# A two-layer hybrid backbone on one core: merged triangular inverses, attention in units of two heads, and separate buffers for the first weights of layer 1

## The chip, the core and the metric

The kernel runs on one core of one Trainium2 chip. The metric is the device time of one execution, in microseconds (us). The engines are TensorE (PE in the profile; its weight loads are PEld), VectorE (DVE), ScalarE (ACT), GpSimd (POOL) and SyncE (SP). Each works through its own queue in order.

## The reference

Two layers act on 512 latent tokens and 256 context tokens of width 1024, in float32. Each layer normalises and modulates the tokens, projects them once, and gives the columns to three mixers whose outputs are concatenated and projected out; then a feed-forward network (layer 0) or a top-2-of-8 mixture of experts (layer 1) follows. In layer 1 only the latents are carried on. The two mixers that the change touches:

```python
# attention: 8 query heads, 2 key/value heads of width 64
s = jnp.einsum('bqkgd,bskd->bkgqs', qi, k).astype(F32) * scale
p = jax.nn.softmax(s, axis=-1).astype(v.dtype)
return jnp.einsum('bkgqs,bskd->bqkgd', p, v)
...
# gated delta rule, 4 heads, chunks of 64, forward and backward
lower = jnp.where(strict, beta[..., :, None] * kk * decay, 0.0)
sol = lax.linalg.triangular_solve(jnp.eye(cs, dtype=F32) + lower, rhs,
                                  left_side=True, lower=True, unit_diagonal=True)
```

Latents attend to all 768 tokens, context tokens (layer 0 only) to the 256 of the context.

## The kernel before, in words

Full-precision products are made of three matmuls of operands that were split into a high and a low part (`parts`, L205: ScalarE writes the high part, VectorE subtracts for the low one). `weights` (L166) opens the buffers for raw and split weights, `load` (L193) has SyncE fetch one, `split` (L199) splits it. Per layer the program runs as follows.

1. `project` (L575) makes the projections: the head columns of three groups (`heads`, `group`; matmuls L220 to L222), channel columns (`feat`; L214 to L216), the gates and the gram matrices of the delta rule. In layer 0 the first group's weights are loaded in advance; in layer 1 they are loaded in `heads(1, w0)`, with `w0` empty, into the buffers that `k.weights(es, 5, pa, 2)` opens. These lie where the residual stream x of the feed-forward part was.
2. `solve` (L1521) inverts the unit triangular 32x32 blocks of all chunks and heads. `solve1` (L1661) does one direction: four 32x1024 transposes (L1672) bring the blocks into one lane each (`tt`), then for each of 30 pivots a multiply (L1681) and an add (L1682) follow, then a 128x1024 transpose back (L1685). The two directions are run in step (`zip`), so their instructions alternate. They all have a high priority in the scheduler.
3. Attention is a generator (L1432) of which one step is run after every second (layer 0) or third (layer 1) pivot, and the rest during the delta-rule steps. One step takes one head and one pair of query tiles of 128: `scores` (L1473) makes S on TensorE (L1483, L1484), VectorE takes the row maximum (L1485) and negates it (L1486), ScalarE takes the exponential with the row sums (L1487), VectorE the reciprocal (L1488), and P is multiplied by it, on VectorE (L1490) or ScalarE (L1492) as `DVE_SCALE` says. `values` (L1451) works one step later: transposes of P (L230), copies of them (L1457), products with V in two column halves of the array (L1461), the sum of the two halves (L1464 on ScalarE, L1466 on VectorE). Query tiles: 48 in layer 0 (8 heads x 6), 32 in layer 1 (8 x 4).
4. `merge` (L1703) builds 64x64 inverses, and `stage2` (L1739) runs the 12 steps of the delta rule in both directions: r (L1777, or for a chunk by a GpSimd-issued transfer L1778), products with the inverse (L1784), the decay matrices (L1800, on GpSimd in layer 0) and so on. Steps of attention stand between them.
5. `tail` projects out and runs the feed-forward part.

A tile scheduler fixes the order of instructions on each engine when the program is built, from priorities; buffers come from pools, and an instruction waits until its buffer's last reader is done.

## Time and profile before

| | |
|---|---|
| median of 3 runs | 2194.21 us (2187.08 to 2195.78) |
| the profiled execution | 2191.7 us |
| span of its trace | 2190.1 us |
| TensorE busy | 2033.4 us (93%) |
| VectorE busy | 1473.6 us (67%) |
| ScalarE busy | 1010.3 us (46%) |
| GpSimd busy | 157.5 us (7%) |
| mean granted TensorE clock | 0.970 |

Busy times are averages over stages with different limits, so the change is to be read in its own stages: projections and inverses of layer 0 to about 275 us, its merge and delta-rule steps to 446, the start of layer 1 at 1126 to 1157, its inverses to 1390 and its steps to 1497. A TensorE record can contain waiting, since matmuls are pipelined and their ends are modelled.

### The profile page before, as it was taken

The page shows a single profiled execution, that of the slowest core. Times are in us where ns is not written, and L with a number is a line of the kernel's source. Part 1 is how long each engine was busy: PE and PEld are TensorE (multiplying, and loading weights), DVE is VectorE, ACT ScalarE, POOL GpSimd, SP SyncE. Part 2 cuts the span into 40 slices and gives each one's busy share as a digit, 9 for nine tenths or more (in the row PEclk, how much of TensorE's full clock was granted, in tenths as well). Part 3 has the DMA queues.
Part 4 walks back from the last instruction along what each step waited for, and adds up shares of the span by engine and source line. Part 5 has one row for each costly group of instructions (what it writes and reads, how often), then busy time and mean ns, then how long its engine had stood idle before and what let it go on. Part 6 is the DMA issues. An engine that isn't in the chain of part 4 may idle for free. (4 is left out here: it accounts for less than half of the span.)

```text
span 2190.1 us, 33735 instructions
## 1 busy us (share of the span) xinstructions
PE 2033.4 (93%) x12390; PEld 1647.6 (75%) x12390; DVE 1473.6 (67%) x2857; ACT 1010.3 (46%) x1764; POOL 157.5 (7%) x226
## 2 busy tenths in 40 slices
PE   6999999988999999999969997899889999999995
PEld 2988766776888888888849875677667777777774
DVE  4859967766885624242366599787667788766776
ACT  3664386633322222222235544753455576655554
POOL 0000201100000000000000003110020000000011
PEclk9999999999999999999979999998999999999998
DMA  6332544152554515131313223106597799667783
GB/s 259 98 120 64 170 159 159 36 190 80 185 193 153 179 29 198 48 97 44 107 33 103 97 89 94 40 30 210 178 267 274 238 353 347 208 234 231 245 289 127
DMA packets 120755, 342.47 MB, mean 156 GB/s; under 512 B 13104, under 2 KB 34592, under 8 KB 120576
## 3 DMA queue, kind: packets, MB, share of 16 engines
q1 hardware_dynamic: 80064, 271.75, 36.9%
q0 software_dynamic: 15248, 49.97, 6.8%
q10 hardware_dynamic: 25264, 18.42, 2.7%
q8 instruction: 106, 1.74, 0.3%
q14 instruction: 73, 0.60, 0.1%
HBM read 304.95 MB, written 35.14 MB: 155 GB/s over the span
## 5 line engine op out<-in xcount | busy, mean ns | idle before, releaser
L206 ACT ACTIVATE hi<-raw 128x1024 fp32r<-128x1024 f32 (+3 forms) x444 | 426.5, 986 | 333.9 <-PE ps L215 255.2
L207 DVE TENSOR_TENSOR lo<-raw,hi 128x1024 fp32r<-128x1024 f32 (+3 forms) x444 | 494.9, 1134 | 90.7 <-ACT hi L206 76.8
L214 PE MATMUL ps<-hh,hi 128*128 128x512 f32 (+1 forms) x1040 | 356.3, 343 | 0.5 <-ACT hi L206 0.5
L216 PE MATMUL ps<-hh,lo 128*128 128x512 f32 (+1 forms) x1040 | 354.6, 341 | 2.0 <-DVE lo L207 2.0
L215 PE MATMUL ps<-hl,hi 128*128 128x512 f32 (+1 forms) x1040 | 355.2, 342 | 0.0
L216 PEld LDWEIGHTS ps<-hh,lo 128*128 128x128 f32 x1040 | 198.6, 191 | 24.6 <-DVE lo L207 2.8
L214 PEld LDWEIGHTS ps<-hh,hi 128*128 128x128 f32 x1040 | 198.8, 191 | 24.1 <-ACT hi L206 1.6
L215 PEld LDWEIGHTS ps<-hl,hi 128*128 128x128 f32 x1040 | 198.8, 191 | 21.6
L222 PE MATMUL ps<-lo,xh 128*128 128x512 f32 (+1 forms) x384 | 150.3, 392 | 11.2 <-DVE lo L207 5.9
L220 PE MATMUL ps<-hi,xh 128*128 128x512 f32 (+1 forms) x384 | 145.5, 379 | 1.0 <-ACT hi L206 0.8
L221 PE MATMUL ps<-hi,xl 128*128 128x512 f32 (+1 forms) x384 | 144.2, 376 | 0.0
L1267 DVE TENSOR_TENSOR sg<-sg,ps 128x512 f32<-128x512 f32 (+1 forms) x44 | 24.3, 553 | 153.8 <-PE ps L216 153.8
L215 PE MATMUL ps<-gl,hi 128*128 128x256 f32 (+1 forms) x352 | 119.4, 339 | 0.0
L214 PE MATMUL ps<-gh,hi 128*128 128x256 f32 (+1 forms) x352 | 118.9, 338 | 0.0
L216 PE MATMUL ps<-gh,lo 128*128 128x256 f32 (+1 forms) x352 | 118.5, 337 | 0.0
L222 PEld LDWEIGHTS ps<-lo,xh 128*128 128x128 f32 x384 | 72.0, 188 | 40.5 <-DVE lo L207 18.7
L220 PE MATMUL ps<-hi,hh 128*128 128x400 f32 (+2 forms) x272 | 92.0, 338 | 10.9 <-ACT hi L206 10.7
L295 DVE SCALAR_TENSOR_TENSOR macc<-mraw,sT,macc 128x512 f32<-128x512 f32 x112 | 80.0, 747 | 16.7 <-DMA mraw<-wmod 16.2
L222 PE MATMUL ps<-lo,hh 128*128 128x400 f32 (+2 forms) x272 | 89.0, 329 | 0.1
L221 PE MATMUL ps<-hi,hl 128*128 128x400 f32 (+2 forms) x272 | 88.8, 327 | 0.0
L783 DVE SCALAR_TENSOR_TENSOR xr<-ps,modc,xr 128x512 f32<-128x512 f32 (+1 forms) x80 | 49.1, 615 | 51.8 <-PE ps L216 51.7
L220 PEld LDWEIGHTS ps<-hi,xh 128*128 128x128 f32 x384 | 72.3, 188 | 14.4 <-ACT hi L206 2.4
(556 smaller groups left out, 4189.1 us busy)
## 6 DMA issues: line engine op xcount, KB each, us to landing
raw<-wmg SPq DMA_DIRECT2D x176, 512.0 KB
raw<-wmd SPq DMA_DIRECT2D x80, 512.0 KB
raw<-wmod SPq DMA_DIRECT2D x52, 512.0 KB
raw<-wgu SPq DMA_DIRECT2D x44, 512.0 KB
mraw<-wmod SPq DMA_DIRECT2D x44, 512.0 KB
raw<-wout SPq DMA_DIRECT2D x32, 512.0 KB
raw<-wt SPq DMA_DIRECT2D x24, 512.0 KB
raw<-wd SPq DMA_DIRECT2D x32, 256.0 KB
```

The lines of the kernel that those rows point to most:

```text
L206: self.nc.scalar.activation(hi, src, AF.Copy)
L207: self.nc.vector.tensor_sub(lo, src, hi.bitcast(F32))
L214: mm(out, wh, xh, start=start, stop=False)
L215: mm(out, wh, xl, start=False, stop=False)
L216: mm(out, wl, xh, start=False, stop=stop)
L220: mm(out, xh, wh, start=start, stop=False)
L221: mm(out, xl, wh, start=False, stop=False)
L222: mm(out, xh, wl, start=False, stop=stop)
L295: nc.vector.scalar_tensor_tensor(a, w, c, a, op0=OP.mult, op1=OP.add)
L783: nc.vector.scalar_tensor_tensor(x[d][:, o:o + n], p[:, :n], k.modc[l][:, s, 40 + d:41 + d], x[d][:, o:o + n], op0=OP.mult, op1=OP.add)
L1267: nc.vector.tensor_mul(s, s, pu)
```

## The change

- *Inverses.* `solve1` handles both directions at once: `tt` has two halves, one multiply (L1721 of the new file) and one add (L1722) per pivot work on both by a two-step access pattern. Four ScalarE copies per layer put the blocks side by side so that one 128x1024 transpose (L1702) fills the lanes of a direction.
- *Attention.* One unit is two heads and a pair of query tiles. The query side is scaled by −0.125 and not 0.125, so that the row minimum is the bias and the exponential takes the scale −1: the negation goes. P isn't normalised. After a unit's scores the reciprocals of its four row-sum columns are taken in one instruction, GpSimd multiplies them into four diagonal 128x128 blocks (`a_dg`, L1477), and in `values` two matmuls of ones with them spread the reciprocals over 64 partitions each; ScalarE copies that (`a_rs`) and VectorE multiplies it into the output. The two heads use the two column halves, so no sum of halves is left. `a_q` and `a_p` get 4 and 6 buffers.
- *First weights of layer 1.* Group 1 gets raw and split buffers of its own, opened on the other side, and `heads(1, w0)` comes ahead of the pool for the norm tiles.

```diff
@@ weights, load, split @@
-    def weights(self, es, n, pool, raw=3):
+    def weights(self, es, n, pool, raw=3, cols=1024):
+        self.wcols = cols
-        raw = self.wraw.tile([128, 1024], F32, name="raw")
+        raw = self.wraw.tile([128, self.wcols], F32, name="raw")
-        hi = self.whl[0].tile([128, 1024], F32R, name="hi")[:, :n]
-        lo = self.whl[1].tile([128, 1024], F32R, name="lo")[:, :n]
+        hi = self.whl[0].tile([128, self.wcols], F32R, name="hi")[:, :n]
+        lo = self.whl[1].tile([128, self.wcols], F32R, name="lo")[:, :n]
@@ layer @@
-                k.weights(es, 0, pa, 4)
+                k.weights(es, 0, pa, 3)
@@ project @@
     with ep or ExitStack() as es:
+        ew = ExitStack()
         if ep is None:
+            k.weights(ew, 4, pb, 4, 2 * WGN[1])
+            w0 = group_weights(k, l, 1)
             k.weights(es, 5, pa, 2)
         k.banks(es, pt=3, pg=2, ps=3)
         cv = pa(es, "cv", 2)
...
                 bg.append((mix.heads(mx, i), 1))
+            heads(1, w0)
+            ew.close()
             with ExitStack() as e5:
                 g.norm_tiles(pa(e5, "p0"), cv)
-                heads(1, w0)
                 for m in range(4):
                     job(g.channel(m, feat))
                 tile_ = group(0)
@@ heads (q side) @@
-        nc.vector.tensor_scalar(st[:, :, 0:4], st[:, :, 0:4], 0.125, None, op0=OP.mult)
+        nc.vector.tensor_scalar(st[:, :, 0:4], st[:, :, 0:4], -0.125, None, op0=OP.mult)
@@ queries, attention, turn, values, scores @@
+    def queries(self, h):
+        qs = [self.pool.tile([128, T], F32R, name="a_q", bufs=4) for _ in range(2)]
+        for i, q in enumerate(qs):
+            self.k.nc.gpsimd.dma_start(q[:, :self.w], self.qs[h + i, :, :self.w])
+        return qs
     def attention(self, sp, cat, groups):
         k, nc = self.k, self.k.nc
...
+        w, late, n = self.w, None, 0
         for g in range(2):
             kh, v = self.first if g == 0 else self.keys(g)
...
+            for h in (4 * g, 4 * g + 2):
+                q = self.queries(h) if h else self.q0
+                yb = sp.tile([128, w], F32, name="a_y", bufs=1)
                 for pair in range(2 if self.last else 3):
                     kts = list(range(NT)) if pair < 2 else [4, 5]
...
+                    st = sp.tile([128, 3, 4], F32, name="a_st", bufs=3)
+                    P, pt = [], []
+                    for i in range(2):
+                        P.append(self.scores(sp, q[i], kh, pair, kts, st, 2 * i))
+                        if late:
+                            self.turn(sp, i, *late)
+                        if late and i:
+                            self.values(sp, cat, *late)
+                        yield
+                        n += 1
+                        if groups and n % 3 == 0:
+                            k.mod(0, groups.pop(0), "t", "t")
+                    late = h, pair, kts, P, v, yb, st, pt
+        for i in range(2):
+            self.turn(sp, i, *late)
+        self.values(sp, cat, *late)
+    def turn(self, sp, j, h, pair, kts, P, v, yb, st, pt):
+        k, nc = self.k, self.k.nc
+        pt.append(sp.tile([128, NT, 256], F32, name="a_pt"))
+        for a in range(0, len(kts), 2):
+            tp = k.transposes([P[j][i][:, b * 128:b * 128 + 128] for b in (a, a + 1) for i in range(2)], b="t")
+            tp = tp.rearrange("p (t q) -> p t q", t=2)
+            (nc.vector.tensor_copy if DVE_COPY[self.l] and a == 2 else nc.scalar.copy)(pt[j][:, kts[a]:kts[a] + 2], tp)
+        if j:
+            dg = sp.tile([128, 4, 128], F32, name="a_dg", bufs=1)
+            nc.vector.reciprocal(st[:, 2], st[:, 1])
+            nc.gpsimd.tensor_mul(dg, k.C("ident").unsqueeze(1).to_broadcast([128, 4, 128]),
+                                 st[:, 2].unsqueeze(2).to_broadcast([128, 4, 128]))
+            pt.append(dg)
+    def values(self, sp, cat, h, pair, kts, P, v, yb, st, pt):
         k, nc, w = self.k, self.k.nc, self.w
...
         op = k.psum("t")
         for a, t in enumerate(kts):
...
+            for j in range(2):
+                nc.tensor.matmul(op[64 * j:64 * j + 64, :256], v[:, t], pt[j][:, t], start=a == 0, stop=a == len(kts) - 1,
+                                 tile_position=(0, 64 * j))
+        for j in range(2):
+            nc.tensor.matmul(op[64 * j:64 * j + 64, 256:], k.C("ones")[:, :64],
+                             pt[2][:, 2 * j:2 * j + 2].rearrange("p i q -> p (i q)"), start=True, stop=True, tile_position=(0, 64 * j))
+        rs = sp.tile([128, 256], F32, name="a_rs", bufs=1)
+        nc.scalar.activation(rs, op[:, 256:], AF.Copy)
+        nc.vector.tensor_mul(yb[:, pair * 256:pair * 256 + 256], op[:, :256], rs)
         if pair == (1 if self.last else 2):
...
+            if 2 + h // 2 in cat:
                 k.parts(yb[:, :w], *cat[2 + h // 2])
...
+            else:
                 nc.gpsimd.dma_start(self.cat[2 + h // 2, :, :w], yb[:, :w])
...
+    def scores(self, sp, q, kh, pair, kts, st, c):
         k, nc = self.k, self.k.nc
...
         o, n = kts[0] * 128, len(kts) * 128
...
+        Ps = []
+        for i in range(2):
+            lq = q[:, (2 * pair + i) * 128:(2 * pair + i) * 128 + 128]
+            P = sp.tile([128, T], F32, name="a_p", bufs=6)
+            s = k.psum("S")
+            for a in range(0, n, 512):
+                m = min(512, n - a)
+                nc.tensor.matmul(s[:, a:a + m], lq, kh[0][:, o + a:o + a + m], start=True, stop=False)
+                nc.tensor.matmul(s[:, a:a + m], lq, kh[1][:, o + a:o + a + m], start=False, stop=True)
+            nc.vector.tensor_reduce(st[:, 0, c + i:c + i + 1], s[:, :n], axis=AX.X, op=OP.min)
+            nc.scalar.activation(P[:, :n], s[:, :n], AF.Exp, bias=st[:, 0, c + i:c + i + 1], scale=-1.0, accum_out=st[:, 1, c + i:c + i + 1])
+            Ps.append(P)
+        return Ps
@@ solve @@
             yield
     def solve(self, sp):
-        both = zip(self.solve1(sp, 0), self.solve1(sp, 1))
+        both = self.solve1(sp)
         while True:
             with self.k.tc.high_priority(offset=-AHEAD[self.l]):
-                if next(both, None) is None:
+                if next(both, self) is self:
                     return
             yield
@@ solve1 @@
...
+    def solve1(self, sp):
         k = self.k
         nc = k.nc
...
+        tt = sp.tile([128, 2, 32, 32], F32, name="tt", bufs=1)
+        tmp = sp.tile([128, 2, 240], F32, name="tm", bufs=1)
+        bb = sp.tile([128, 2, 32], F32, name="bb", bufs=1)
+        nb = sp.tile([128, 2, 32], F32, name="nb", bufs=1)
+        for d in range(2):
+            u = slice(24 * d, 24 * d + 32)
+            for c in range(2):
+                q = slice(c * 64 + 32 - 32 * d, c * 64 + 64 - 32 * d)
+                nc.scalar.copy(self.kt[q, 24 * d:24 * d + 24, 32 * d:32 * d + 32], self.kt[q, 24 * d:24 * d + 24, 32 - 32 * d:64 - 32 * d])
+            nc.vector.transpose(out=tt[:, d], in_=self.kt[:, u, 32 * d:32 * d + 32].rearrange("p u i -> p i u"))
+            nc.vector.transpose(out=bb[:, d], in_=self.beta[:, u])
         nc.vector.tensor_scalar(nb, bb, -1.0, None, op0=OP.mult)
...
+        nc.vector.tensor_mul(tt, tt, nb.unsqueeze(3).to_broadcast([128, 2, 32, 32]))
+        nc.vector.memset(tt.rearrange("p d i c -> p d (i c)")[:, :, ::33], 1.0)
+        def both(a, b):
+            assert [list(x) for x in a.ap] == [list(x) for x in b.ap]
+            return bass.AP(tensor=a.tensor, offset=a.offset, ap=[a.ap[0], [b.offset - a.offset, 2]] + list(a.ap[1:]))
         for s in range(1, 31):
...
+            n, j = 31 - s, 31 - s
+            sh = [128, 2, n, s]
+            rows, cols = (slice(s + 1, 32), slice(0, n)), (slice(0, s), slice(32 - s, 32))
+            t = tmp[:, :, :s * n].rearrange("p d (i c) -> p d i c", c=s)
+            x = both(tt[:, 0, rows[0], cols[0]], tt[:, 1, rows[1], cols[1]])
+            piv = both(tt[:, 0, rows[0], s:s + 1], tt[:, 1, rows[1], j:j + 1])
+            row = both(tt[:, 0, s:s + 1, cols[0]], tt[:, 1, j:j + 1, cols[1]])
+            nc.vector.tensor_mul(t, piv.to_broadcast(sh), row.to_broadcast(sh))
+            nc.vector.tensor_add(x, x, t)
             yield
...
+        nc.vector.tensor_mul(tt, tt, bb.unsqueeze(2).to_broadcast([128, 2, 32, 32]))
+        for d in range(2):
+            nc.vector.transpose(out=self.tb[:, d].rearrange("p u i -> p i u"), in_=tt[:, d])
         yield
```

How the order moves, at three places. First VectorE in layer 0, where the transposes into lanes (`tt<-kt`) and the pivots (`tm` and `tt`; L1681, L1682 before, L1721, L1722 now) stand; before, from the first transpose, and the middle of the pivots:

```order
L1672 STREAM_TRANSPOSE tt_2535<-kt 32x1024
L1320 TENSOR_REDUCE m_s<-sq 128x6
L1672 STREAM_TRANSPOSE tt_2535<-kt 32x1024 x3
L1320 TENSOR_REDUCE m_s<-sq 128x6
L1673 STREAM_TRANSPOSE bb_2537<-beta 128x32
L207 TENSOR_TENSOR lo<-raw,hi 128x1024 x2
L1674 TENSOR_SCALAR nb_2538<-bb_2537 128x32
L1672 STREAM_TRANSPOSE tt_2549<-kt 32x1024
...
L1681 TENSOR_TENSOR tm_2536<-tt_2535 128x240
L1681 TENSOR_TENSOR tm_2550<-tt_2549 128x238
L1682 TENSOR_TENSOR tt_2535<-tt_2535,tm_2536 128x16x15
L1682 TENSOR_TENSOR tt_2549<-tt_2549,tm_2550 128x17x14
```

Now:

```order
L1703 STREAM_TRANSPOSE bb<-beta 128x32 x2
L1704 TENSOR_SCALAR nb<-bb 128x64
L1326 TENSOR_REDUCE m_s<-sq 128x6
L1702 STREAM_TRANSPOSE tt<-kt 128x1024 x2
L1705 TENSOR_TENSOR tt<-tt,nb 128x2048
L1326 TENSOR_REDUCE m_s<-sq 128x6
...
L393 SCALAR_TENSOR_TENSOR cv<-cv,vec 128x255
L1721 TENSOR_TENSOR tm<-tt 128x2x198
L395 SCALAR_TENSOR_TENSOR cv<-cv,vec 128x255
L208 TENSOR_TENSOR m_hl<-m_x,m_hl 128x4x64
L1722 TENSOR_TENSOR tt<-tt,tm 128x2x22x9
```

Eight transposes of 32 partitions became two of 128, and where a direction's instruction stood between the other's, convolution or split instructions of the projection now stand between multiply and add.

Second ScalarE at the start of layer 1: `hh` are the modulated tokens (512 latents, then 256 of the context), `sq` and `pv` the norm, and `hi<-raw 128x512` the splits of group 1's weights. Before:

```order
L366 ACTIVATE hh_5021<-ht,modc_75 128x512
L343 ACTIVATE pv<-pn 128x256
L366 ACTIVATE hh_5014<-ht,modc_75 128x256
...
L366 ACTIVATE hh_5020<-ht,modc_75 128x256
L366 ACTIVATE hh_5021<-ht,modc_75 128x256
L206 ACTIVATE hi<-raw 128x512 x4
```

Now:

```order
L207 ACTIVATE hi<-raw 128x512
L367 ACTIVATE hh_4776<-ht,modc_75 128x512
L367 ACTIVATE hh_4777<-ht,modc_75 128x512
L207 ACTIVATE hi<-raw 128x512 x3
L367 ACTIVATE hh_4778<-ht,modc_75 128x512
...
L367 ACTIVATE hh_4783<-ht,modc_75 128x512
L339 ACTIVATE sq<-xr_4803 128x256
L339 ACTIVATE sq<-xr_4807 128x256
L344 ACTIVATE pv<-pn 128x256
L367 ACTIVATE hh_4776<-ht,modc_75 128x256
```

The four splits stood behind the last context tile and stand ahead of, or among, the first latent ones.

Third GpSimd in the delta-rule steps of layer 1: `r` are the transfers of a step, `go_z` those of the output gate, `qd` products, `a_dg` the new diagonals. Before:

```order
L1778 DMA r_13385<-tok_10548 128x4x64
L1851 DMA go_z<-z_10552 64x2x256
L1778 DMA r_13388<-tok_10548 128x4x64
L1778 DMA r_13533<-tok_10548 128x4x64
L1778 DMA r_13536<-tok_10548 128x4x64
L1778 DMA r_13708<-tok_10548 128x4x64
L1803 TENSOR_TENSOR qd<-qtok,egc 128x256 x2
L1778 DMA r_13711<-tok_10548 128x4x64
L1778 DMA r_13885<-tok_10548 128x4x64
```

Now:

```order
L1819 DMA r_12975<-tok_10310 128x4x64
L1819 DMA r_12978<-tok_10310 128x4x64
L1819 DMA r_13106<-tok_10310 128x4x64
L1819 DMA r_13109<-tok_10310 128x4x64
L1819 DMA r_13286<-tok_10310 128x4x64
L1819 DMA r_13289<-tok_10310 128x4x64
L1477 TENSOR_TENSOR a_dg<-cst,a_st 128x512
L1844 TENSOR_TENSOR qd<-qtok,egc 128x256 x2
L1477 TENSOR_TENSOR a_dg<-cst,a_st 128x512
L1819 DMA r_13444<-tok_10310 128x4x64
```

Diagonals now stand in the queue behind the transfers of later steps.

## Rows read from the trace of the kernel before

**Rows 1.** Busy time by stretch: start:end, length, PE, PEld, DVE, ACT, POOL, clock, DMA share, GB/s.

```profile
174.00:252.00 78.00, 74.25 (x432) 65.80 (x431) 77.75 (x190) 27.62 (x50) 9.70 (x11) 0.96 0.34 104
252.00:275.00 23.00, 18.20 (x111) 12.25 (x111) 21.49 (x58) 12.65 (x25) 6.28 (x7) 0.85 0.60 209
275.00:320.00 45.00, 41.68 (x407) 30.56 (x406) 28.75 (x76) 40.43 (x81) 1.90 (x4) 1.00 0.46 166
320.00:446.00 126.00, 119.36 (x1182) 88.73 (x1180) 96.65 (x268) 86.14 (x203) 24.74 (x40) 0.97 0.31 106
1263.00:1328.00 65.00, 56.51 (x290) 48.29 (x289) 62.52 (x144) 23.15 (x42) 7.63 (x10) 0.97 0.38 114
1328.00:1407.00 79.00, 64.21 (x484) 45.94 (x483) 68.55 (x169) 54.76 (x107) 12.04 (x16) 0.94 0.17 51
1407.00:1497.00 90.00, 80.95 (x906) 66.28 (x905) 74.19 (x192) 46.65 (x107) 17.17 (x31) 0.91 0.24 75
```

**Rows 2.** Instruction groups by shape, triangular inverses: total us, mean ns, idle before.

```profile
L1672 DVE STREAM_TRANSPOSE tt<-kt 32x1024 f32<-32x1024 f32 x16 | 32.1, 2007 | 0.3
L1685 DVE STREAM_TRANSPOSE tb<-tt 128x1024 f32<-128x1024 f32 x4 | 7.9, 1972 | 0.0
L1681 DVE TENSOR_TENSOR tm<-tt 128x240 f32<-128x240 f32 x8 | 3.0, 397 | 0.0
L1681 DVE TENSOR_TENSOR tm<-tt 128x30 f32<-128x30 f32 x8 | 1.5, 188 | 0.0
```

**Rows 3.** Timeline of VectorE, dense pivots of two directions (start, length).

```profile
220.92 0.39 DVE L1681 TENSOR_TENSOR tm<-tt 128x108 f32<-128x108 f32 x2
```

**Rows 4.** Timeline of VectorE, a chain in which each needs the one before.

```profile
1129.38 0.16 DVE L244 SCALAR_TENSOR_TENSOR rqus<-rqus,rqxs 128x2 f32<-128x2 f32 x1
1129.57 0.16 DVE L245 SCALAR_TENSOR_TENSOR rqis<-rqus,rqis 128x2 f32<-128x2 f32 x1
```

**Rows 5.** Instruction groups by shape, VectorE, attention.

```profile
L1490 DVE TENSOR_SCALAR a_p<-a_p,a_st 128x768 f32<-128x768 f32 x48 | 32.9, 685 | 0.4
L1486 DVE TENSOR_SCALAR a_st<-a_st 128x1 f32<-128x1 f32 x80 | 11.1, 142 | 0.6
L1488 DVE RECIPROCAL a_st<-a_st 128x1 f32<-128x1 f32 x80 | 12.6, 158 | 9.2 <-ACT a_p L1487 8.4
L1466 DVE TENSOR_TENSOR a_y<-t,a_lo 64x256 f32<-64x256 f32 x40 | 16.6, 414 | 7.5 <-ACT a_lo L1464 6.8
```

**Rows 6.** Instruction groups by shape, ScalarE: attention, and a half-width copy.

```profile
L1492 ACT ACTIVATE a_p<-a_p,a_st 128x768 f32<-128x768 f32 x16 | 15.0, 935 | 3.4 <-DVE a_st L1488 3.2
L1464 ACT ACTIVATE a_lo<-t 64x256 f32<-64x256 f32 x40 | 15.2, 381 | 17.0 <-PE t L1461 16.2
L1714 ACT COPY tinv<-tb 32x1536 f32<-32x1536 f32 x8 | 11.8, 1471 | 1.8 <-DVE tb L1685 1.7
```

**Rows 7.** Timeline at the start of layer 1: TensorE, ScalarE, SyncE queue.

```profile
1142.07 0.58 PE L220 MATMUL ps<-hi,hh 128*128 128x256 f32 x1 [9.36 <-ACT hi L206]
1156.77 0.40 PE L214 MATMUL ps<-hh,hi 128*128 128x512 f32 x1
...
1141.38 0.63 ACT L206 ACTIVATE hi<-raw 128x512 fp32r<-128x512 f32 x1 [1.66 <-DMA raw<-wg]
...
1138.85 5.08 SPq L195 DMA_DIRECT2D raw<-wg  x4
```

**Rows 8.** Waits of GpSimd, 320 to 446, then 1328 to 1497 us (total, times, longest).

```profile
POOL r L1778 <- PE pg L1784: 47.8, 7, 14.5
...
POOL r L1778 <- PE pg L1784: 33.7, 4, 10.6
```

**Rows 9.** Timeline of GpSimd and VectorE side by side, and the group mean.

```profile
322.07 1.36 POOL L1800 TENSOR_TENSOR ad<-cst,al 128x256 f32<-128x256 f32 x2
322.29 0.67 DVE L1803 TENSOR_TENSOR qd<-qtok,egc 128x256 f32<-128x256 f32 x1
...
L1777 DVE TENSOR_TENSOR r<-ktok,egc 128x256 f32<-128x256 f32 x24 | 10.3, 432 | 3.0 <-PE pg L1784 2.9
```

More of the change, by code (lines that the diff above doesn't have):

```diff
@@ L1413, in preload @@
         self.pool = pool
-        self.first, self.q0 = self.keys(0), self.query(0)
+        self.first, self.q0 = self.keys(0), self.queries(0)
     def keys(self, g):
@@ L1434, in attention @@
         for g in range(2):
             kh, v = self.first if g == 0 else self.keys(g)
-            for h in range(4 * g, 4 * g + 4):
-                q = self.q0 if h == 0 else self.query(h)
-                if h % 2 == 0:
-                    yb = sp.tile([128, w], F32, name="a_y", bufs=1)
+            for h in (4 * g, 4 * g + 2):
+                q = self.queries(h) if h else self.q0
+                yb = sp.tile([128, w], F32, name="a_y", bufs=1)
                 for pair in range(2 if self.last else 3):
@@ L1441, in attention @@
                     kts = list(range(NT)) if pair < 2 else [4, 5]
-                    P = [self.scores(sp, q, kh, pair * 2 + i, kts) for i in range(2)]
-                    if late:
-                        self.values(*late)
-                    late = sp, h, pair, kts, P, v, yb, cat
-                    yield
-                if groups:
-                    k.mod(0, groups.pop(0), "t", "t")
-        self.values(*late)
-    def values(self, sp, h, pair, kts, P, v, yb, cat):
-        k, nc, w = self.k, self.k.nc, self.w
-        pt = sp.tile([128, NT, 256], F32, name="a_pt")
-        for a in range(0, len(kts), 2):
-            tp = k.transposes([P[i][:, b * 128:b * 128 + 128] for b in (a, a + 1) for i in range(2)], b="t")
-            tp = tp.rearrange("p (t q) -> p t q", t=2)
-            (nc.vector.tensor_copy if DVE_COPY[self.l] and a == 2 else nc.scalar.copy)(pt[:, kts[a]:kts[a] + 2], tp)
+                    st = sp.tile([128, 3, 4], F32, name="a_st", bufs=3)
@@ L1466, in values @@
-        nc.vector.tensor_add(yb[hb:hb + 64, pair * 256:pair * 256 + 256], op[0:64, :256], lo)
+            for j in range(2):
[4 more added lines that the diff above has]
+                             pt[2][:, 2 * j:2 * j + 2].rearrange("p i q -> p (i q)"), start=True, stop=True, tile_position=(0, 64 * j))
@@ L1475, in scores @@
         k, nc = self.k, self.k.nc
-        lq = q[:, qt * 128:qt * 128 + 128]
         o, n = kts[0] * 128, len(kts) * 128
-        P = sp.tile([128, T], F32, name="a_p", bufs=4)
-        st = sp.tile([128, 4], F32, name="a_st", bufs=3)
-        s = k.psum("S")
-        for a in range(0, n, 512):
-            m = min(512, n - a)
-            nc.tensor.matmul(s[:, a:a + m], lq, kh[0][:, o + a:o + a + m], start=True, stop=False)
-            nc.tensor.matmul(s[:, a:a + m], lq, kh[1][:, o + a:o + a + m], start=False, stop=True)
```

43 lines of the change are left out of this document (1 added, 42 removed).

## The prediction

> **What bounds the kernel now.** I read the table of busy time by stretch first. The reader is to see that three stages have three different limits [rows 1]. While the triangular inverses run (174 to 252 in layer 0, 1263 to 1328 in layer 1), VectorE is busy for 77.75 of 78 us and 62.52 of 65 us: it sets the end there, and TensorE, with 74.25 and 56.51, is the next limit. Attention by itself in layer 0 (252 to 320) is first VectorE's (21.49 of 23), then, beside the merge, ScalarE's (40.43 of 45). In layer 1 attention and the rest of the inverses (1328 to 1407) are VectorE's (68.55 of 79). In the delta-rule steps with attention between them (320 to 446 and 1407 to 1497) no engine but TensorE is near full, and TensorE's records overlap with waiting, so I take those stretches as a chain of short dependent steps that other work delays.
>
> The second view is the timeline at the start of layer 1 [rows 7]. TensorE stands idle 9.36 us until 1142.07, for the first weights of group 1. SyncE issued their transfer only at 1138.85, because their buffers lie where the residual x was still being read; ScalarE splits the first at 1141.38. The head matmuls then last until the first channel matmul at 1156.77, 14.7 us.
>
> **Own first weights.** The four weights of group 1 now have buffers of their own, and the rows of ScalarE's order show their splits ahead of the context's norm, not behind it. TensorE's order is unchanged (context norm, heads, channel), so the heads can start at the end of the idle time, 1142.07 − 9.36 = 1132.7. The channel's first weight still waits for x (1138.85, then split some 2.5 us later, as the first weight was), which is earlier than 1132.7 + 14.7 = 1147.4. I take the whole idle time, **−9.4 us**. Ends: 0 if something else holds the heads, and −15 if the heads also run shorter, since the channel's weight cannot be split before 1138.85 + 2.5 = 1141.4 and 1156.77 − 1141.4 = 15.4.
>
> **Transposes.** Each layer had eight 32x1024 transposes of 2.007 us and gets two 128x1024 ones, whose nearest rows are the ones at the end of the same routine, 1.972 us [rows 2]: 16.06 − 3.94 = 12.1 us less of VectorE a layer. Added are four ScalarE copies of 32x768 a layer, half of the 1.471 us of a 32x1536 copy [rows 6], so about 0.74 us each; two stand ahead of the first transpose, 1.5 us, while VectorE has convolutions and weight splits to do. Where VectorE sets the end, 12.1 comes out whole; but TensorE leaves only 78 − 74.25 = 3.75 us in layer 0 and 65 − 56.51 = 8.5 us in layer 1 [rows 1] if its busy time were all work, and some of it is waiting. Between 3.75 and 12.1 I take **−7**, between 8.5 and 12.1 **−10**.
>
> **Pivots.** 120 instructions a layer become 60 with twice the elements. At 240 elements one takes 397 ns, at 30 it takes 188 [rows 2]: (397 − 188)/210 = 0.995 ns an element and 158 ns fixed. So a merged one of 216 elements takes 158 + 215 = 373 ns. But the two directions were independent and overlapped: two multiplies of 108 took 0.39 us together [rows 3]. Merged, each add needs its multiply, and dependent VectorE instructions start 0.19 us apart where one lasts 0.16 [rows 4], so 0.373 + 0.03 = 0.40 stands against 0.39. I take **0**. Ends: +1.5 us a layer if no other instruction fills the gap, −5 if the projection's instructions that the new order puts between them hide it and one start of about 0.08 us a pair is saved.
>
> **Attention.** P is no longer divided by its sum; the division comes as a 128x256 multiply of the output, by reciprocals that a diagonal (GpSimd) and ones-matmuls (TensorE) spread over the partitions. The normalisations were VectorE's for one query tile of each pair in layer 0 (ScalarE's for the other) and for all in layer 1. VectorE, layer 0: 16 normalisations × 0.685, 48 negations × 0.142, 36 of 48 reciprocals × 0.158, 12 of 24 output instructions × 0.414 [rows 5] = 11.0 + 6.8 + 5.7 + 5.0 = 28.5 us. Layer 1: 32 × 0.685 + 32 × 0.142 + 24 × 0.158 + 8 × 0.414 = 33.5. ScalarE: layer 0 16 × 0.935 + 12 × 0.381 [rows 6] = 19.6; layer 1 only 8 × 0.381 = 3. (The 256-column normalisations of layer 0 are left out; they are small.) TensorE gets two matmuls a unit, 40 in all, in front of an output that it computed anyway.
>
> By stage, with the query tiles that fall there (counted by their row-maximum instructions, one a tile, in the instruction groups of each stretch): layer 0 before 320 has 22 of 48, so 13.1 us of VectorE and 9.0 of ScalarE; ScalarE is the fuller, **−9** (ends −4 and −13). Layer 0's steps have the other 15.4 us of VectorE, not near full (96.65 of 126): two fifths, **−6** (0 to −15). Layer 1 before 1407 has 24 of 32, 25.1 us; TensorE leaves 79 − 64.21 = 14.8 [rows 1], and ScalarE, little relieved, takes over next: **−10** (−2 to −15). Layer 1's steps, 8.4 us: **−3** (−8, or +4 as the last unit's transposes and copies come for two heads at once).
>
> **The diagonals.** 20 GpSimd multiplies of 128x512 are new. GpSimd's 128x256 one takes 0.68 us (1.36 for two), and the VectorE multiply that began 0.22 us into it took 0.67 us against a mean of 0.432 for its shape [rows 9]: 0.24 us lost. 20 × 0.24 = 4.8; part of it on slack: **+3**. Ends 0, and 20 × 1.36 = 27 if each held VectorE for its whole length. The Trainium skill ("SBUF — State Buffer", section "Who interferes with whom") says that a VectorE instruction with two SBUF inputs and a GpSimd instruction that reads SBUF fully block each other for a whole instruction. By that rule the diagonals cost up to the 27 us and the change brings half; the trace agrees in that the 0.67 us instruction ended with GpSimd's, but the pivots and splits it would hit are only part of VectorE's stream.
>
> **Sum.** −9.4 − 7 − 10 + 0 − 9 − 6 − 10 − 3 + 3 = −51.4 us. The profiled execution took 2191.7 us, 2.5 below the median of 2194.21, so **2140**.
>
> **The rivals.**
> *Attention is not the limit* (16 in 100): the steps of the delta rule and ScalarE hold every stage after the inverses, and only the boundary and the transposes count: 2191.7 − 9.4 − 17 = 2165. For it: 119.36 of 126 us of TensorE in layer 0's steps. Against it: VectorE's 68.55 of 79 in layer 1.
> *Every VectorE instruction pays its fixed part* (6 in 100): then 60 fewer save 60 × 0.158 = 9.5 us a layer, in layer 0 some 2 of it before TensorE limits: 2129. Against it stands the pair of 0.39 us. The Trainium skill ("VectorE: DVE Perf Modes", section "The DRAIN you can't avoid") says that the next instruction does not start until the pipe is empty; the trace differs here, as two that last 158 + 107 = 265 ns each took 0.39 us together.
> *GpSimd's queue holds the diagonals* (slower, 5 in 100). It works in order, and its r transfers wait for TensorE: 7 waits of 47.8 us in layer 0's steps (longest 14.5), 4 of 33.7 in layer 1's (longest 10.6) [rows 8]. In the new order eight of the diagonals stand right behind an r transfer, four a layer; TensorE, in order too, then stops at the ones-matmul. At the longest wait each, 4 × 14.5 + 4 × 10.6 = 100 us, 2140 + 100 = 2240. At the mean (6.8 and 8.4) it is 61 us, 2201, no difference: that, or most terms at their weak ends, has 7 in 100. It decides from 51.4/8 = 6.4 us a diagonal on. Against it: a unit's diagonal has a whole unit's scores ahead of its use.
> *The boundary does not move* (2 in 100): 2150.
>
> **How the numbers follow.** The forecast has 64 in 100. The favourable ends together (−15, −12, −12, pivots −10, −13, −15, −15, −8) give 2191.7 − 100 = 2092; all weak ends together end above 2200, so I stop the range at 2098 and 2182, which takes in the rivals at 2165, 2150 and 2129 and leaves out those at 2201 and 2240 and the tails. Faster by over 0.5% (11 us, about what a measurement of this kernel can tell) 88 in 100, within 7, slower 5.
>
> **What would show it.** Right: TensorE's idle time before the heads of layer 1 gone; the transposes 3.9 us a layer; merged pivots of 480 elements at about 0.63 us; VectorE below full in the inverses, and the stretches before 320 and 1407 some 10 us shorter each. Wrong: ones-matmuls as the place where TensorE waits longest, on a diagonal behind an r transfer; two-input VectorE instructions at twice their length beside the diagonals; ScalarE full from the first score to the last output.

## The result and the profile after

The changed kernel takes 2158.19 us (median; 2157.22 to 2161.2), the one before 2193.56 in the same comparison: a ratio of 0.9852, 95% interval 0.9833 to 0.987, so 32 us or 1.5% less. The forecast was 2140, range 2098 to 2182: direction and range hold, but 18 us of the gain are missing. The profiled execution took 2161.2 us, its span is 2159.5, 30.6 below the span of before.

The table gives landmarks of the traces, as differences to the kernel before: when the inverses, steps and output projections of each layer begin or end. The steps' begin is the first VectorE product `L<-ktok,ekd`; the scheduler can move that instruction, so it is a weaker mark than the others. A trace is one execution, and its time can lie some microseconds off the median (5.7 us below it for a_only, 8.4 for b_only, two kernels of the next section), so whole times are compared by the ratios, and places by the traces. Places drift too: the first transpose of layer 0 lies between 171.7 and 178.2 us in the traces of this document, though little ahead of it differs, so differences in layer 0 are also counted from its first score.

| | before, us | changed, difference |
|---|---|---|
| layer 0: first score on TensorE | 252.7 | −7.2 |
| layer 0: inverses end | 274.6 | −7.6 |
| layer 0: delta-rule steps begin | 320.4 | −14.7 |
| layer 0: last attention output | 432.6 | +6.2 |
| layer 0: output projection begins | 446.4 | −0.6 |
| layer 1: first channel matmul | 1156.8 | −11.6 |
| layer 1: first transpose into lanes | 1263.0 | −5.0 |
| layer 1: first score | 1326.8 | −15.6 |
| layer 1: steps begin | 1407.3 | −35.0 |
| layer 1: output projection begins | 1496.6 | −33.5 |

So layer 0 gained 14.7 us up to its steps and lost 14.1 of them inside the steps. From its first score to its output projection it takes 200.3 us, where it took 193.7. What is left comes from the start of layer 1 and from layer 1, and 3 us of it are given back behind layer 1's output projection.

The table of busy time by stretch of the changed kernel answers to [rows 1]; its columns are the same, and the stretches are moved to the new landmarks:

```profile
174.00:246.00 72.00, 70.45 (x429) 63.03 (x428) 69.65 (x137) 30.11 (x52) 5.66 (x10) 1.00 0.41 123
246.00:267.00 21.00, 14.83 (x109) 9.92 (x108) 14.35 (x17) 8.77 (x18) 6.45 (x6) 0.84 0.69 245
267.00:306.00 39.00, 37.82 (x356) 27.30 (x356) 16.87 (x32) 29.40 (x61) 11.55 (x14) 1.00 0.40 134
306.00:446.00 140.00, 132.02 (x1277) 96.33 (x1273) 89.31 (x211) 77.36 (x192) 31.24 (x44) 0.99 0.31 103
1258.00:1311.00 53.00, 51.65 (x273) 43.56 (x272) 52.07 (x103) 25.59 (x44) 8.06 (x10) 1.00 0.47 144
1311.00:1372.00 61.00, 55.20 (x447) 42.59 (x446) 43.62 (x64) 44.86 (x88) 17.48 (x22) 0.94 0.22 66
1372.00:1463.00 91.00, 86.97 (x1005) 71.11 (x1002) 70.67 (x166) 50.37 (x116) 20.29 (x32) 0.96 0.26 81
```

The reader is to see two things. In the inverses (first and fifth line) VectorE is still full, and TensorE's busy time now nearly fills them too (70.45 of 72, 51.65 of 53): as far as it is work, the next limit is reached. The granted clock of TensorE is 1.00 in both, where [rows 1] has 0.96 and 0.97. In layer 0's steps (fourth line) the stretch became longer, 140 us and not 126, though VectorE fell from 96.65 to 89.31 us and ScalarE from 86.14 to 77.36.

Instruction groups of VectorE in the changed kernel, to be held against [rows 2, 5]:

```profile
L1702 DVE STREAM_TRANSPOSE tt<-kt 128x1024 f32<-128x1024 f32 x4 | 7.9, 2019 | 0.6 <-ACT kt L1701 0.6
L1726 DVE STREAM_TRANSPOSE tb<-tt 128x1024 f32<-128x1024 f32 x4 | 7.7, 1967 | 3.0 <-DMA cat<-cv 3.0
L1721 DVE TENSOR_TENSOR tm<-tt 128x480 f32<-128x480 f32 x4 | 2.6, 658 | 0.1
L1722 DVE TENSOR_TENSOR tt<-tt,tm 128x480 f32<-128x480 f32 x4 | 2.6, 658 | 0.1
L1494 DVE TENSOR_TENSOR a_y<-t,a_rs 128x256 f32<-128x256 f32 x20 | 8.4, 418 | 18.0 <-ACT a_rs L1493 17.8
```

Transposes into lanes take 2.019 us for 128 partitions where four of 2.007 stood: 12.0 of the 12.1 us a layer are there. A merged pivot of 480 elements takes 658 ns (worked out: 636), two for a pivot.

The start of layer 1, timelines of TensorE and of SyncE's queue, to be held against [rows 7]:

```profile
1128.98 1.19 PE L357 MATMUL pn<-dg,cst 128*128 128x256 f32 x2 [3.88 <-DVE dg L352]
1136.69 0.38 PE L221 MATMUL ps<-hi,hh 128*128 128x256 f32 x1 [1.43 <-DVE ht L362]
1145.19 0.40 PE L215 MATMUL ps<-hh,hi 128*128 128x512 f32 x1
...
1098.04 1.75 SPq L196 DMA_DIRECT2D raw<-wg  x4
1136.31 0.80 SPq L196 DMA_DIRECT2D raw<-wt  x2
```

The weights of group 1 are issued at 1098 and not at 1138.85. TensorE goes from the context's norm into the heads without the 9.36 us. At 1136.69 it waits 1.43 us for modulated tokens, and the first channel matmul comes at 1145.19, 11.6 us earlier.

### The profile page after: what moved, and what is told of

Same layout as the page of the kernel before. It is cut to its first block, busy times and chain, and to the rows that moved or that the text cites. A ratio compares the mean times of both kernels' runs of the same rounds, so it can differ in the third digit from the quotient of the medians.

```text
span 2159.5 us, 33553 instructions
## 1 busy us (share of the span) xinstructions
PE 2027.9 (94%) x12470; PEld 1648.4 (76%) x12470; DVE 1401.9 (65%) x2501; ACT 990.2 (46%) x1728; POOL 179.9 (8%) x246
## 5 line engine op out<-in xcount | busy, mean ns | idle before, releaser
L223 PEld LDWEIGHTS ps<-lo,xh 128*128 128x128 f32 x384 | 72.4, 189 | 37.6 <-DVE lo L208 15.6
L1515 DVE TENSOR_REDUCE a_st<-S 128x1 f32<-128x768 f32 (+1 forms) x80 | 66.2, 844 | 33.9 <-PE S L1514 33.5
L296 DVE SCALAR_TENSOR_TENSOR macc<-mraw,sT,macc 128x512 f32<-128x512 f32 x112 | 80.0, 747 | 12.0 <-DMA mraw<-wmod 11.3
L1516 ACT ACTIVATE a_p<-S,a_st 128x768 f32<-128x768 f32 (+1 forms) x80 | 65.2, 817 | 45.8 <-DVE a_st L1515 40.5
```

What stands on the lines that cost most here:

```text
L223: mm(out, xh, wl, start=False, stop=stop)
L296: nc.vector.scalar_tensor_tensor(a, w, c, a, op0=OP.mult, op1=OP.add)
L1515: nc.vector.tensor_reduce(st[:, 0, c + i:c + i + 1], s[:, :n], axis=AX.X, op=OP.min)
L1516: nc.scalar.activation(P[:, :n], s[:, :n], AF.Exp, bias=st[:, 0, c + i:c + i + 1], scale=-1.0, accum_out=st[:, 1, c + i:c + i + 1])
```

## The experiments

**Each part alone.** Three kernels take one part of the change each into the kernel before, a fourth takes all but the attention.

```diff
 a_only: solve and solve1 of the change, in the kernel before
 b_only: attention, turn, values, scores, queries, the scale -0.125
         and k.weights(es, 0, pa, 3) of the change, in the kernel before
 c_only: weights, load, split and the head of project of the change, in the kernel before
 no_b:   a_only and c_only together
```

> The kernel before with the merged triangular inverses alone; attention and the first weights of layer 1 are as before. Theory 1 (each part keeps what its own stage gains): 7 us less in layer 0 and about 10 in layer 1, 17 in all, 2176. Theory 2 (what layer 0 gains ahead of its delta-rule steps is lost in them, because attention sets their end): the inverses of layer 0 end 7 us earlier, but the output projection of layer 0 starts at the same 446 us; only layer 1's 10 us are left, 2183.

> The kernel before with two-head attention alone (normalisation of the output in place of P's); inverses and first weights are as before. Theory 1 (the new units are better everywhere except in the delta-rule steps of layer 0, which they lengthen): about 7 us less before the steps of layer 0, 14 more in them, 10 to 20 less in layer 1: 2175 to 2190. Theory 2 (the steps of layer 0 lengthen only because they begin earlier, and the output projection of layer 0 keeps its start at 446 us): layer 0 as before, layer 1 10 to 20 us less, 2173 to 2183. The two differ in where the output projection of layer 0 starts: some 453 us by theory 1, 446 by theory 2.

> The kernel before with own buffers for the first weights of layer 1 alone. Theory 1 (as in the changed kernel's trace: the heads 11 us earlier, the channel stretch behind them 4.4 us longer because its weights cannot come earlier): 7 us less, 2186. Rival (the idle time of 9.4 us is the whole of it and nothing is given back): 9 to 12 us less, 2182 to 2184.

> The changed kernel with the attention of before (inverses merged, own first weights). Theory 1 (parts add): 17 + 7 = 24 us less than before, 2169, and attention's part of the change is the other 11 us. Theory 2 (layer 0's gain lost in its steps): 17 less, 2176, and attention's part is 18 us. If it is at 2158 or below, the new attention brings nothing.

| kernel | median, us | ratio to before | 95% interval |
|---|---|---|---|
| inverses alone (a_only) | 2164.28 | 0.9881 | 0.9855 to 0.9908 |
| attention alone (b_only) | 2179.39 | 0.9949 | 0.993 to 0.9967 |
| first weights alone (c_only) | 2184.32 | 0.9979 | 0.9964 to 0.9994 |
| all but the attention (no_b) | 2157.55 | 0.9843 | 0.9815 to 0.9871 |
| the whole change | 2158.19 | 0.9852 | 0.9833 to 0.987 |

The inverses alone bring 1.2% (26 us), more than the 17 and the 10 that the two theories expected. The kernel without the new attention is as fast as the whole change: on top of the other two parts the attention brings nothing. In its trace the output projection of layer 0 begins at 435.0 us, in the changed kernel at 445.8; layer 1 takes 20.0 us less than before from its first transpose to its output projection, in the changed kernel 28.5. The new attention brings some 8 us in layer 1 and costs 11 in layer 0. Theory 2 falls: with the inverses alone the output projection of layer 0 does come 11.9 us earlier. Theory 1 has the places right, and b_only's projection begins 5.3 us late, where it said about 7. The first weights bring 0.2% (4.6 us, interval 1 to 8), nearer to the 7 of what is given back than to the 9 to 12 of the rival.

**Which half of the inverses.**

```diff
 a1_transposes, in solve1 of the kernel before
-        for q in range(4):
-            s, o = slice(q * 32, q * 32 + 32), (q % 2) * 32
-            nc.vector.transpose(out=tt[s], in_=self.kt[s, 24 * d:24 * d + 32, o:o + 32]...)
+        for c in range(2):
+            q = slice(c * 64 + 32 - 32 * d, c * 64 + 64 - 32 * d)
+            nc.scalar.copy(self.kt[q, ..., 32 * d:32 * d + 32], self.kt[q, ..., 32 - 32 * d:64 - 32 * d])
+        nc.vector.transpose(out=tt, in_=self.kt[:, 24 * d:24 * d + 32, 32 * d:32 * d + 32]...)
 a2_pivots: merged pivots, but the eight transposes of before
```

> The kernel before with one 128x1024 transpose a direction alone (and its two ScalarE copies); the two directions keep their own pivots. The inverses alone gave 25 us of the times of before (33 us between the profiled spans). Theory X (VectorE's time is all of it: 12.1 us less a layer, which comes out whole): 20 to 25 us below before. Theory Y (merging the directions is half of it: in the trace of before the last multiply and transpose of the second direction end 14.6 us after those of the first, behind attention): 10 to 15 us below before.

> The kernel before with merged pivots alone: both directions in one instruction, still eight 32x1024 transposes into lanes. Theory X: no difference to before, within 4 us, since the merged instructions take VectorE as long as the pairs did (28.7 to 31.0 us against 29.2 to 32.7 a layer). Theory Y: 10 to 15 us below before, with the end of the inverses of layer 0 some 12 us earlier.

Transposes alone: 2169.61 us, ratio 0.9903 (0.9875 to 0.9931), 21 us. Merged pivots alone: 2189.96 us, ratio 1.0005 (0.9993 to 1.0018), nothing. Theory X holds in both. The pivots are worth nothing, as worked out ahead, and the transposes most of their 2 x 12.1 us. That both halves together gave 26 us and the transposes 21 lies within the intervals.

**Where layer 0 loses it.** The change also takes one of four buffers from the weights of the modulation (wmod), which are loaded and used during layer 0's attention, since the six a_p buffers need the room. no_b_raw3 does that to the kernel with the old attention; mix01 keeps the old attention in layer 0 (with four weight buffers) and the new one in layer 1.

```diff
 no_b_raw3, on no_b
-                k.weights(es, 0, pa, 4)
+                k.weights(es, 0, pa, 3)
 mix01, on the changed kernel: class HeadMix(Mix) with attention, values, scores of before
...
-        g, mix = Gdn(k, l, gp), Mix(k, l, last)
+        g, mix = Gdn(k, l, gp), (Mix if last else HeadMix)(k, l, last)
...
-                k.weights(es, 0, pa, 3)
+                k.weights(es, 0, pa, 4)
...
-        nc.vector.tensor_scalar(st[:, :, 0:4], st[:, :, 0:4], -0.125, None, op0=OP.mult)
+        nc.vector.tensor_scalar(st[:, :, 0:4], st[:, :, 0:4], -0.125 if self.l else 0.125, None, op0=OP.mult)
```

> The changed kernel with the attention of before, and with three buffers for the modulation weights that are loaded during layer 0's attention, as the change has them, where the attention of before had four. Theory 1 (the modulation matmuls of layer 0 wait for their weights: 22.1 us of TensorE from one start to the next in the changed kernel's layer 0, 14.7 with four buffers): 4 to 8 us above the kernel with old attention and four buffers, 2162 to 2165. Theory 2 (TensorE lost the time to the ones-matmuls, 8.1 us, and to the order of the units): no difference, 2157.

> The changed kernel with the attention of before in layer 0 and the new attention in layer 1. From the traces: the new attention costs layer 0 11 us (output projection at -0.6 against -11.4 us) and brings layer 1 8.5 us (28.5 against 20 from its first transpose to its output projection). If layers don't interact, 8 to 11 us below the changed kernel: 2147 to 2150. If the new attention does nothing for layer 1 either and the difference is in the layer's start, 2157.

The third buffer costs far more than expected: 2179.63 us, ratio 0.9961 (0.994 to 0.9982), where no_b has 2157.55: 22 us by the medians, 26 by the ratios. mix01 takes 2146.68 us, ratio 0.9802 (0.9781 to 0.9824): 11 us below the changed kernel, as expected, and its interval lies below that of the change. SyncE's queue (the wmod loads: start, length, number) and TensorE's matmuls with them (t<-raw,sT, from 245 to 450 us), first with four buffers (no_b), then with three (no_b_raw3), then the changed kernel:

```profile
247.23 122.52 SPq L196 DMA_DIRECT2D raw<-wmod  x28
...
L265 PE MATMUL t<-raw,sT 128*32 128x512 f32 x112 | 14.7, 599 | 0.0
```

```profile
251.07 150.25 SPq L196 DMA_DIRECT2D raw<-wmod  x28
...
L265 PE MATMUL t<-raw,sT 128*32 128x512 f32 x112 | 20.7, 601 | 0.6 <-DMA raw<-wmod 0.4
```

```profile
245.63 150.85 SPq L196 DMA_DIRECT2D raw<-wmod  x28
...
L265 PE MATMUL t<-raw,sT 128*32 128x512 f32 x112 | 23.3, 644 | 1.5 <-DMA raw<-wmod 1.5
```

With four buffers the 28 loads are issued within 122.52 us, with three within 150.25 and 150.85. The 112 records are the same, but TensorE is busy with them for 20.7 and 23.3 us, not 14.7. It hardly waits for a transfer there (0.4 and 1.5 us). What it loses shows in the two timelines of SyncE's queue and TensorE at one of the seven groups, first no_b, then no_b_raw3:

```profile
247.23 1.75 SPq L196 DMA_DIRECT2D raw<-wmod  x4
270.99 1.92 PE L265 MATMUL t<-raw,sT 128*32 128x512 f32 x16
```

```profile
251.07 1.28 SPq L196 DMA_DIRECT2D raw<-wmod  x3
274.71 1.91 PE L265 MATMUL t<-raw,sT 128*32 128x512 f32 x12
275.80 1.28 SPq L196 DMA_DIRECT2D raw<-wmod  x3
281.20 1.05 PE L265 MATMUL t<-raw,sT 128*32 128x512 f32 x4
```

A group needs four weights. With four buffers all four are there ahead of time, and its 16 records run as one in 1.92 us. With three, the fourth weight is issued only when the group's own matmuls have begun; its four records come later, behind other matmuls, and take another 1.05 us. All seven groups are split like that with three buffers, in no_b_raw3 and in the changed kernel, and one of seven in no_b: some 6 us of TensorE. The last attention output comes 9.9 us later (434.1 against 424.2); 3.8 of that is there at the first score already (250.9 against 247.1), so 6.1 us arise behind it.

**The new attention with four buffers.** If a unit's transposes stand ahead of the next unit's scores, four a_p buffers do, and the room gives the fourth weight buffer back. A third kernel leaves the whole normalisation out in layer 0: the diagonals, the ones-matmuls, and ScalarE's copies of their result. What follows then works on other numbers, so it is read up to the output projection of layer 0.

```diff
 tf_raw4, on the changed kernel (tf_raw3 without the last line)
-                        P.append(self.scores(sp, q[i], kh, pair, kts, st, 2 * i))
                         if late:
                             self.turn(sp, i, *late)
+                        P.append(self.scores(sp, q[i], kh, pair, kts, st, 2 * i))
-            P = sp.tile([128, T], F32, name="a_p", bufs=6)
+            P = sp.tile([128, T], F32, name="a_p", bufs=4)
-                k.weights(es, 0, pa, 3)
+                k.weights(es, 0, pa, 4)
 no_ones0, on the changed kernel, layer 0 alone
-        if j:
+        if j and self.last:
...
-            nc.tensor.matmul(op[64 * j:64 * j + 64, 256:], k.C("ones")[:, :64],
...
-        nc.vector.tensor_mul(yb[:, pair * 256:pair * 256 + 256], op[:, :256], rs)
+        if self.last:
...
+        else:
+            nc.vector.tensor_copy(yb[:, pair * 256:pair * 256 + 256], op[:, :256])
```

> The changed kernel with a unit's transposes put ahead of the next unit's scores, which lets a_p do with 4 buffers in place of 6; the room gives layer 0's modulation weights their fourth buffer back. Theory 1 (the new attention lost its gain in layer 0 to the missing weight buffer): the output projection of layer 0 starts 10 us or more before the changed kernel's 445.8 us, and the time is 2145 to 2150, like the kernel with the old attention in layer 0. Theory 2 (the ones-matmuls and the units themselves cost TensorE the time): no earlier than 443, 2155 to 2160.

> As the kernel before this one, with the three weight buffers of the change: it shows what the order of transposes and scores does by itself. Theory 1: within 5 us of the changed kernel, 2153 to 2163, and 8 us or more above the same kernel with four buffers. Theory 2: the same as with four buffers.

> The changed kernel without the normalisation of layer 0's attention: no diagonals, no ones-matmuls, and the output is copied where it was multiplied. What follows in layer 1 then works on other numbers, so it is read up to the output projection of layer 0. Theory 1 (the weight buffer): the output projection starts within 3 us of the changed kernel's 445.8 us. Theory 2 (8.1 us of ones-matmuls on TensorE are on the path): 437 to 440.

| kernel | median, us | ratio to before | 95% interval | last attention output | output projection of layer 0 |
|---|---|---|---|---|---|
| tf_raw4 | 2146.79 | 0.9806 | 0.9781 to 0.9832 | 432.5 | 439.5 |
| tf_raw3 | 2176.56 | 0.9938 | 0.9912 to 0.9963 | 444.2 | 471.0 |
| no_ones0 | 2155.22 | 0.9836 | 0.9806 to 0.9866 | 432.5 | 439.9 |
| the whole change | 2158.19 | 0.9852 | 0.9833 to 0.987 | 438.8 | 445.8 |

The same two views of tf_raw4, then of tf_raw3:

```profile
247.40 122.00 SPq L196 DMA_DIRECT2D raw<-wmod  x28
...
L265 PE MATMUL t<-raw,sT 128*32 128x512 f32 x112 | 18.7, 646 | 5.3 <-DVE a_pt L1472 5.3
```

```profile
246.95 155.40 SPq L196 DMA_DIRECT2D raw<-wmod  x28
...
L265 PE MATMUL t<-raw,sT 128*32 128x512 f32 x112 | 24.9, 610 | 7.7 <-DVE a_pt L1472 3.9 <-DMA raw<-wmod 3.8
```

tf_raw4's time is what theory 1 said (2145 to 2150), but its projection begins 6.3 us earlier than the changed kernel's, not 10 or more: theory 1 is not the whole of it. The buffer is worth 30 us between these two. 11.7 of them come before the last attention output (12.2 counted from the first score), where it was 9.9 (6.1) with the old attention. The rest arises behind it: in tf_raw3 (and in no_b_raw3) the scheduler put ScalarE's split of c6, the first operand of the output projection, behind the outputs of the delta rule, and TensorE waits for it:

```profile
471.04 1.22 PE L215 MATMUL ps<-c6h,hi 128*128 128x512 f32 x2 [5.45 <-ACT c6h L207]
```

tf_raw3 is 18 us slower than the change, where theory 1 expected no difference. That is this place: from the last attention output to the projection it takes 26.8 us, the change 7.0. In the change the split is not late, so there I count 6 to 12 us for the buffer, carried over from the two pairs; the change with nothing but a fourth buffer was not run. Theory 2 is right in part. Without the normalisation the output projection begins 5.9 us earlier (expected 6 to 9), 8.1 counted from the first score. That is the price of diagonals, ones-matmuls and copies together; no run has the ones-matmuls out alone. Even with four buffers the new attention's projection begins at 439.5, the old one's at 435.0 (no_b) and 433.1 (mix01). The ones-matmuls are twice as many records as I had counted, 80 for 40 matmuls; the group in the changed kernel, then its part in layer 0 (245 to 446 us):

```profile
L1490 PE MATMUL t<-a_dg,cst 128*64 128x256 f32 x80 | 15.5, 380 | 0.0
...
L1490 PE MATMUL t<-a_dg,cst 128*64 128x256 f32 x48 | 8.9, 380 | 0.0
```

**A candidate.** mix_tf puts the old attention into layer 0 and transposes first into layer 1:

> A candidate made of what the runs left best in each layer: the changed kernel with the attention of before in layer 0 (and four weight buffers), and in layer 1 the new attention with a unit's transposes ahead of the next unit's scores and four a_p buffers. From the traces: layer 0 with the old attention brings 13.3 us up to its output projection; layer 1 with the transposes first took 33.9 us less than before from its first transpose to its output projection, against 27.9 in the other order. If these hold together, 2141 to 2143. If the order in layer 1 matters only because of what layer 0 leaves behind, 2146 to 2148.

It takes 2146.07 us, ratio 0.9788 (0.9759 to 0.9817), which cannot be told from mix01 and tf_raw4. The three are about 2% below the kernel before and some 11 us below the change, and I would keep mix01 or tf_raw4. The 2141 to 2143 of two gains that add did not come. In its trace both are nearly there: the output projection of layer 0 begins at 434.8, and layer 1 takes 33.7 us less than before from its first transpose to its output projection. But behind that it takes 697.5 us, where mix01 takes 695.0 and the kernel before 693.5. So that the order in layer 1 brings something in the whole time is not shown.

## Why the prediction was right, and where it was not

*Own first weights, −9.4.* The mechanism was right: the idle time went, and the first channel matmul came 11.6 us earlier. But the end of the first four channels, 1192.0 before and 1184.8 now, is only 7.2 us earlier. It is not their weights, as I expected for c_only: those are issued earlier too (from 1136.31, before from 1146.93). TensorE now waits for the convolution of a channel, 1.97 us for ScalarE and 0.44 for VectorE, where it did not wait before:

```profile
1164.71 0.88 PE L231 MATMUL pg<-cst,cv 128*128 128x128 f32 x6 [1.97 <-ACT cv L1571]
```

Right behind that wait its granted clock fell to the lower level (1.2 GHz) for a time: 0.95 from 1145 to 1168 us and 0.97 to 1188, where the same matmuls had 1.00 before. The kernel with this part alone gained 4.6 us, half of the term.

*Transposes, −7 and −10.* Right up to the first score, too small in all: alone they gave 21 us, where I had cut 24.2 to 17 for TensorE's sake. The stretch from the first transpose to the first score, which the two terms were worked out for, fell from 78.7 to 71.6 us in layer 0 and from 63.8 to 54.8 in layer 1 in the trace of a1_transposes (71.2 and 53.2 in the changed kernel), so by 7.0 and 9.1. The rest came behind it, which I had put at nothing: the inverses of layer 0 end at 254.3 and not at 274.6 us, and from the first score to the output projection a1_transposes took 3.5 us less in layer 0 and 7.3 less in layer 1. TensorE's busy time was no floor: from the first transpose to the first score of layer 0 it fell from 74.9 to 69.9 us with VectorE's. Its clock may have a part in that: in the four traces with eight transposes a layer the granted clock of these stretches is 0.95 to 0.97, in those with two 0.98 to 1.00. What the clock alone was worth is not shown.

*Pivots, 0.* Right: 1.0005 alone. The rival by which every VectorE instruction pays its fixed part (9.5 us a layer) falls with it. What "The DRAIN you can't avoid" in the Trainium skill's "VectorE: DVE Perf Modes" says of the next instruction waiting for an empty pipe would have made this part faster. But the section also says that an instruction which is not held starts earlier. Two independent ones overlapped here (0.39 us for a pair), so joining them gains nothing.

*Attention before the steps, −9 and −10; in layer 1's steps −3.* In layer 1 the steps begin 8.1 us earlier, counted from the first score, than with the old attention (−19.4 against −11.3), near the −10; in its steps nothing more came. In layer 0 the −9 was wrong: with the old attention the steps begin 7.1 us earlier still. That mark is moved by the scheduler (in no_b_raw3, the slower kernel, it lies 10 us earlier than in no_b), but the whole of layer 0 says the same: from the first score to the output projection it takes 193.7 us before, 187.9 with the old attention (no_b), and 200.3 with the new.

*Layer 0's steps, −6 (0 to −15).* This is the step that failed: they took 14 us more. I had taken TensorE's 119.36 of 126 us for waiting, and spread VectorE's relief over the stretch. The table of busy time from 300 to 425 us, before and then changed (the same time, not the same work), shows what became of that relief:

```profile
300.00:425.00 125.00, 120.49 (x1150) 86.87 (x1150) 94.88 (x265) 92.65 (x217) 20.53 (x33) 1.00 0.32 112
```

```profile
300.00:425.00 125.00, 119.76 (x1096) 85.25 (x1095) 77.11 (x178) 69.58 (x172) 26.25 (x37) 0.99 0.32 107
```

VectorE fell from 94.88 to 77.11 us and ScalarE from 92.65 to 69.58, and TensorE stayed at 120 of 125, with fewer matmuls done (1096, not 1150). A busy TensorE can be waiting, so this alone doesn't name the limit; the runs do. no_ones0 has the relief and no normalisation, and from its first score to its last attention output it takes 184.8 us; no_b_raw3, with the old attention and the same three weight buffers, takes 183.2. So the relief, with the new order of units, brought nothing, and VectorE and ScalarE were not the limit. Two things that the change put into TensorE's queue did cost: the normalisation with its ones-matmuls, counted in the text of the prediction but priced in no term of the sum (6 to 8 us, by no_ones0), and the split groups of modulation matmuls, from an edit that the diff shows and the prediction never costed, one buffer of four (6 to 12 us, by no_b_raw3 and tf_raw3). Together they are 12 to 20 of the 20 us between −6 and +14; that the buffer costs the changed kernel the same as those two is carried over, not shown.

*The diagonals, +3.* Right in size as VectorE's time; what of it reached the end is not shown, since no run has the diagonals out alone. In the trace six VectorE instructions beside a diagonal took more than their usual time, 4.0 us together. GpSimd's and VectorE's timelines show the plainest:

```profile
1321.41 1.12 POOL L1477 TENSOR_TENSOR a_dg<-cst,a_st 128x512 f32<-128x512 f32 x1 [5.54 <-DVE a_st L1476]
1321.56 1.35 DVE L1721 TENSOR_TENSOR tm<-tt 128x336 f32<-128x336 f32 x1
```

The pivot usually takes 0.51 us, started 0.15 us into the diagonal, and ended 0.38 after it. That is a wait for the diagonal's end, as the Trainium skill ("SBUF — State Buffer", "Who interferes with whom") has it; but with all 20 diagonals of 1.05 us taken whole, 21 us would have gone, and only a fifth of that did.

*GpSimd's queue holds the diagonals.* It was the other way round. GpSimd waited longest on the diagonal itself, which has one buffer, until the ones-matmuls of the unit before had read it, with r transfers behind it:

```profile
POOL a_dg L1477 <- PE t L1490: 46.4, 5, 18.5
POOL r L1819 <- PE pg L1825: 21.5, 4, 10.1
```

Nobody waited for these transfers: among TensorE's waits in layer 0's steps the profile names none for an r transfer and none for a diagonal. The rival's place was right and its price nothing.

*Attention is not the limit* (16 in 100, 2165). This rival came nearer than the forecast, 7 us from the 2158 and not 18: no_b shows that the new attention's part of the change, −25 in the sum with the diagonals, was nothing. Its reason held in part only. In layer 0 relief of VectorE and ScalarE brought nothing, as it says; in layer 1 the new attention did bring 8 us, and layer 0 lost them again.

That the sum came as near as 18 us is in part luck: the inverses alone gave 26 us where their terms had 17, and that covered a third of the gain of attention that did not come. Of the signs named ahead, the idle time gone, the transposes and the merged pivots came as written; VectorE below full in the inverses did not (69.65 of 72 us, 52.07 of 53).

## What to carry to other kernels

Cost every line of a diff, the buffer counts too: here one weight buffer of four was worth more than what the arithmetic that it made room for gained in layer 0. Where a group of matmuls needs four weights, three buffers split every group. Before spreading an engine's relief over a stretch, ask which queue ends it; here, with TensorE at 95% of the stretch, added matmuls cost most of their time (8.9 us of ones-matmuls, 6 to 8 for the normalisation), and a VectorE and ScalarE at some 75% gave nothing back. Joining two independent short VectorE instructions saves nothing where they overlapped already; a transpose that uses 128 partitions and not 32 takes the same 2.0 us, and saves the other three.

## What the runs showed that I had not expected

One buffer less for weights used deep inside another stage cost 22 and 30 us in two pairs of kernels that differ in nothing else, and only 6 to 12 of it, counted from the first score, came up to the last attention output: the rest goes with where the scheduler then placed a later split. A change in a pool's size is also a change in order. And the parts don't add: alone they give 26, 11 and 5 us, 42 together, and the change gives 32.
